# The left factors of the last pair of channel tiles on VectorE instead of GpSimd, and stored at once, in a two-layer decoder trunk on one core

## The chip, the cores and the metric

The kernel runs on one core of a Trainium2 chip. The metric is the device time of one execution in microseconds (us). The kernel before took 2596.47 us (median of three runs, 2592.08 to 2600.52). The execution that was profiled took 2591.86 us, 2590.1 us of it in the span that the trace covers. Engines are named as in the profile: PE is TensorE (PEld its weight loads), DVE VectorE, ACT ScalarE, POOL GpSimd, SP SyncE; SPq is the sequencer of SP, which issues all DMAs named below.

## What is computed

A decoder trunk of two layers over 1024 tokens of width 1024, all in float32. Each layer has an attention part and a gated convolutional FFN; the change lies in the FFN alone, which both layers have:

```python
def conv_ffn(h, w_up, conv_w, conv_b, w_down):
    u = h @ w_up
    C = u.shape[-1]
    u = lax.conv_general_dilated(u, conv_w[:, None, :], window_strides=(1,),
                                 padding=[(CONV_WIDTH - 1, 0)],
                                 dimension_numbers=('NWC', 'WIO', 'NWC'),
                                 feature_group_count=C) + conv_b
    a, b = u[..., :D_FF], u[..., D_FF:]
    return (jax.nn.silu(a) * b) @ w_down
```

`D_FF` is 2816, that is 22 channel tiles of 128.

## The kernel before

**Precision.** Every float32 product on PE is made of three matmuls on split operands (`mm3`, lines 237 to 243): each operand is split into a rounded high half (ACT copies it, line 165) and a low half (DVE subtracts, line 166), and high x high, high x low and low x high are summed in PSUM. In `mm3(out, (lh, ll), (rh, rl))` the first matmul needs both high halves, the second the low half of the right operand, the third the low half of the left operand.

**Up part.** `Up.run` works through the 22 channel tiles `n`. A table of slots (the dictionary `todo`) says when loads, sums, splits, convolution and gate of a tile are issued between its seven products on PE. `Up.gate` (line 1755) makes the hidden tile, 128 channels x 1024 tokens, as one DVE multiplication. Two tiles `g` and `h` form a pair; there are 11 pairs.

**Left factors.** The down projection is done by a seven-product scheme over 2x2 blocks (two halves of the channels, two halves of the tokens), with 11 pairs as its inner steps. Each of the seven products has a left factor per pair: `g[:, :CH]`, `h[:, :CH]`, `s2`, the in-place difference in `g[:, CH:]`, `h[:, CH:]`, `s1` and `s4` (`CH` is 512 tokens). `Up.left` makes four of them with four POOL instructions (lines 1763 to 1766); the other three are halves of the hidden tiles as they are. `Up.store` (line 1772) issues seven DMAs of 256 KB from the SP queue, which put the factors of a pair into DRAM (`gd`, one tensor per pair).

**Down part.** `Down` has 77 steps: product `i` of 7, pair `j` of 11. One step is four PSUM banks x three matmuls of 128x512, twelve matmuls. `Down.prep` loads the left factors of two pairs at a time back from DRAM (`wr<-gd`, line 1860; three buffers), and splits left factor and weight of each step (`wh`, `wl`; four buffers), three steps ahead of PE. Product 0 uses the factor `g[:, :CH]` of every pair. The first steps of product 0 are issued while the last tiles of the up part are still being convolved; its last, step 10, needs pair 10, the last that the up part makes. `Down.claim` loads the weights (`hT`, `hx`, line 1849), and `Down.sums` makes sums of weights on DVE (lines 1881, 1883, 1885) that products 2 to 6 need.

**What sets the order.** Each engine runs its instructions in order, and the SP queue issues DMAs in order: a store that waits holds up the loads behind it. Inside `Up.run` DVE and ACT keep the order in which the code is written (`tc.manual_schedule`); after it, a scheduler orders the instructions of the down part.

Of the diff's lines the ones that matter are these two slots for a pair (`n` odd), and the engine of `Up.left`:

```python
            at(7 * n + 16, self.gate, n)
            if n % 2:
                at(7 * n + 17, self.left, n // 2)
                at(7 * n + 19, self.store, n // 2)
```

Of the kernel before, what the change touches and what calls it, by code (L numbers as in the profile page):

```python
# [30 lines left out]
NF = DFF // P  # L31
# [12 lines left out]
class Plan:  # L44
# [8 lines left out]
    def add(self, eng, us, fn, deps=(), prio=0.0, acq=(), rel=()):  # L53

        t = {"eng": eng, "us": us, "fn": fn, "prio": prio, "acq": acq, "rel": rel, "id": len(self.tasks), "out": []}
        deps = {d["id"]: (d, w) for d, w in (d if isinstance(d, tuple) else (d, 0.1) for d in deps if d is not None)}
        t["wait"] = len(deps)
        for d, w in deps.values():
            d["out"].append((t, w))
        self.tasks.append(t)  # L60
        return t
# [20 lines left out]
    def run(self):  # L82
        engines = ("SP", "POOL", "DVE", "ACT", "PE")
        ready, busy = {e: [] for e in engines}, dict.fromkeys(engines, False)
        events, now, order = [], 0.0, []

        def push(t):
            heapq.heappush(ready[t["eng"]], (t["prio"], t["id"]))
        for t in self.tasks:
            if not t["wait"]:  # L90
                push(t)
        while True:
            for e in engines:
                skipped, q = [], ready[e]
                while q and not busy[e]:
                    x = heapq.heappop(q)
                    t = self.tasks[x[1]]
                    if not self.can(t):
                        skipped.append(x)
                        continue  # L100
                    self.take(t["acq"], 1)
                    order.append(t)
                    busy[e] = e != "SP"
                    heapq.heappush(events, (now + max(t["us"] - self.OVERLAP.get(e, 0.0), 0.0), 0, t["id"]))
                    heapq.heappush(events, (now + t["us"], 1, t["id"]))
                for x in skipped:
                    heapq.heappush(q, x)
            if not events:
                break
            now, kind, i = heapq.heappop(events)  # L110
            t = self.tasks[i]
            if kind == 0:
                busy[t["eng"]] = False
            elif kind == 1:
                self.take(t["rel"], -1)
                for o, w in t["out"]:
                    heapq.heappush(events, (now + w, 2, o["id"]))
            else:
                t["wait"] -= 1
                if not t["wait"]:  # L120
                    push(t)
        assert len(order) == len(self.tasks)
        for t in order:
            t["fn"]()


class Trunk:
# [422 lines left out]
    def attention(self, ap, l, od, units, work, spare, lead=4, lag=2, lead_work=2):  # L550
# [78 lines left out]
        for k in range(first, len(steps) + lag + 4):  # L629
            st = steps[k] if 0 <= k < len(steps) else None  # L630
            run(k, "max")
            if st:
                self.turn_p(ap, st)
                self.upper_p(ap, st)
            run(k, "exp")
            if st:
                self.lower_p(st)
            run(k, "norm")
            while items and items[0]["at"] <= k:
                begin(k, items.pop(0))  # L640
            if k < 0 and lead_work and items:
                for _ in range(lead_work):
                    if work:
                        advance()
            if st and k < n_fill:
                owed += max(total, 0) / (n_fill - k)
                while owed >= 1 and work:
                    owed -= 1
                    advance()
            if 0 <= k - lag < len(steps):  # L650
                for part in range(len(steps[k - lag]["t"])):
                    self.value(steps[k - lag], part)
                if steps[k - lag]["end"]:
                    finish(k, steps[k - lag]["u"])
            if not work and whole and k % 4 == 0:
                operand()
            if k == units[-1]["start"]:
                w_o = self.load_block(self.a["w_o"][l], [(0, CH)])
# [940 lines left out]
class Up:  # L1599
# [158 lines left out]
    def left(self, k):  # L1758

        g, h = self.hidden[2 * k:2 * k + 2]  # L1760
        s1, s2, s4 = (self.k.sb(self.late, [P, CH], F32, "gs", 3) for _ in range(3))
        add = self.k.nc.gpsimd.tensor_tensor
        add(s1, g[:, CH:], h[:, CH:], ALU.add)  # L1763
        add(s2, s1, g[:, :CH], ALU.subtract)
        add(g[:, CH:], g[:, :CH], g[:, CH:], ALU.subtract)
        add(s4, h[:, :CH], s2, ALU.subtract)
        self.factors = (g[:, :CH], h[:, :CH], s2, g[:, CH:], h[:, CH:], s1, s4)
# [7 lines left out]
    def run(self, late, down):  # L1775


        self.late = late
        done = {0: 3, 1: 3}
        self.split_21(1)  # L1780
        self.take_second(0)
        self.take_second(1)
        self.third(1)
        todo = {}

        def at(slot, f, *args):
            todo.setdefault(slot, []).append(lambda: f(*args))
        for slot, f in ((148, down.claim_x), (150, down.claim_x), (152, down.claim_h), (154, down.claim_h), (156, down.claim_h),
                        (158, down.claim_x), (160, down.claim_h)):
            at(slot, f)  # L1790
        at(151, down.fetch, 3)
        for slot, n in ((151, 1), (153, 2), (155, 3), (159, 4)):
            at(slot, down.prep, n)
        for n in range(NF):
            for slot, f in ((-9, self.load), (-6, self.sums_21), (-3, self.sums_34), (-3, self.split_a), (-2, self.split_21),
                            (-1, self.split_b), (3, self.split_34)):
                if n > 1 or n == 1 and f in (self.split_b, self.split_34):
                    at(7 * n + slot, f, n)
            for slot, h, tap in ((11, 0, 1), (12, 0, 0), (13, 1, 1), (14, 1, 0)):
                at(7 * n + slot, self.conv, n, h, tap)  # L1800
            at(7 * n + 16, self.gate, n)
            if n % 2:
                at(7 * n + 17, self.left, n // 2)
                at(7 * n + 19, self.store, n // 2)
        for slot in range(7 * NF + 13):
            for f in todo.pop(slot, ()):
                f()
            for n in (slot // 7 - 1, slot // 7):
                i, odd = divmod(slot - 7 * n, 2)
                if 0 <= n < NF and not odd and done.get(n, 0) <= i < 7:  # L1810
                    self.product(n, i)
            if slot >= 7 * NF + 6:
                down.step()
        assert not todo
# [157 lines left out]
```

## Time and profile before

| | us |
|---|---|
| median of three runs | 2596.47 |
| lowest and highest run | 2592.08, 2600.52 |
| profiled execution, its own time | 2591.86 |
| its span in the trace | 2590.1 |
| busy: PE | 2466.6 (95% of the span) |
| busy: DVE | 1831.0 (71%) |
| busy: ACT | 1339.8 (52%) |
| busy: POOL | 832.7 (32%) |
| DMA queue of the kernel | 43.0% of 16 engines, 355.41 MB |

The table is read from the page of the profile: its first part gives the busy times, its third the DMA queue. The chain of work that ended last is 72% PE, 6% DVE, 6% DMA, 5% ACT and 4% POOL. A busy share is an average over stages with different limits; what one change is worth is read from the stage in which it lies. The two stages here are the ends of the up part, one in each layer, near 1190 us and 2380 us of the span.

### The profile page before, as it was taken

The numbers are of one execution on the slowest core, as the hardware profiler recorded it, in microseconds if no ns is written. First come the engines' busy times: TensorE is split into PE (matmuls) and PEld (weight loads), VectorE is DVE, ScalarE is ACT, GpSimd is POOL, SyncE is SP. The second block draws the span as 40 slices with busy tenths as digits, with TensorE's granted clock in tenths as the row PEclk, the third lists the DMA queues.
The fourth block names the chain that finished last, engine by engine and source line by source line (L and its number), as shares of the span: only waits on it lengthen the run. The fifth ranks groups of instructions, "written<-read, shape, count | busy, mean of one in ns | idle before, by whom it ended". The sixth has DMA issues, their size and how long they took to land.

```text
span 2590.1 us, 35657 instructions
## 1 busy us (share of the span) xinstructions
PE 2466.6 (95%) x12306; PEld 2062.5 (80%) x12306; DVE 1831.0 (71%) x3066; ACT 1339.8 (52%) x2553; POOL 832.7 (32%) x722
## 2 busy tenths in 40 slices
PE   7889999988999999998999999999999999998998
PEld 7778888766778888886889888887777888886886
DVE  5638787666378787877665467878376888787765
ACT  5428787676244544443454356767245454443443
POOL 1335555475134554433000000000233455544000
PEclk9999999999999999999999999999999999999999
DMA  8473233244323333257335466666622333327533
GB/s 251 136 213 86 88 108 104 86 143 134 132 73 98 106 111 101 95 201 254 96 125 155 142 182 192 196 181 177 215 90 78 101 103 110 105 97 281 168 97 114
DMA packets 302700, 357.68 MB, mean 138 GB/s; under 512 B 37960, under 2 KB 183224, under 8 KB 302520
## 3 DMA queue, kind: packets, MB, share of 16 engines
q1 hardware_dynamic: 302520, 355.41, 43.0%
q8 instruction: 97, 1.59, 0.3%
q14 instruction: 83, 0.68, 0.1%
HBM read 245.55 MB, written 109.78 MB: 137 GB/s over the span
## 4 chain that ended last, share of the span: by engine, by line
PE 72%; DVE 6%; DMA 6%; ACT 5%; POOL 4%; issue 2%; SPq 1%; POOLq 0%; ACTq 0%; DVEq 0%
PE psa L241 11%; PE psa L242 11%; PE psa L243 11%; PE psb L241 8%; PE psb L243 8%; PE psb L242 8%; PE psa L384 4%; PE psb L528 4%; PE psb L504 4%; POOL gs L1763 1%; DMA hT<-in_w_down_dram 1%; ACT pt L515 1%; DVE pt L518 1%; DVE ps L414 1%; ACT ps L427 1%
## 5 line engine op out<-in xcount | busy, mean ns | idle before, releaser
L165 ACT ACTIVATE wh<-wr 128x512 fp32r<-128x512 f32 (+2 forms) x240 | 181.8, 760 | 337.1 <-PE psb L243 145.0
L1748 DVE SCALAR_TENSOR_TENSOR v<-u,cw,v 128x1023 f32<-128x1023 f32 (+1 forms) x176 | 282.8, 1607 | 68.7 <-ACT v L1746 67.1
L166 DVE TENSOR_TENSOR wl<-wr,wh 128x512 fp32r<-128x512 f32 (+2 forms) x232 | 223.5, 965 | 148.0 <-ACT wh L165 147.4
L518 DVE TENSOR_TENSOR pt<-psb,pt 128x512 fp32r<-128x512 f32 (+2 forms) x380 | 243.9, 660 | 70.9 <-ACT pt L515 69.3
L1746 ACT ACTIVATE v<-u,cw 128x1024 f32<-128x1024 f32 x88 | 109.6, 1245 | 310.0 <-DVE u L1735 283.3
L515 ACT ACTIVATE pt<-psb 128x512 fp32r<-128x512 f32 (+2 forms) x380 | 212.3, 575 | 108.3 <-PE psb L504 75.9
L528 PE MATMUL psb<-pt,vv 128*128 128x512 f32 (+2 forms) x864 | 244.6, 361 | 12.6 <-DVE pt L518 7.0
L241 PE MATMUL psa<-hT,wh 128*128 128x512 f32 x560 | 218.4, 390 | 5.3 <-DVE u L1709 5.3
L243 PE MATMUL psa<-hT,wl 128*128 128x512 f32 x560 | 218.1, 389 | 0.2 <-DVE wl L166 0.2
L242 PE MATMUL psa<-hT,wh 128*128 128x512 f32 x560 | 217.9, 389 | 0.0
L384 PE MATMUL psa<-kk,qq 128*128 128x512 f32 (+4 forms) x792 | 181.8, 349 | 23.8 <-DMA qq<-qd 11.8
L205 POOL TENSOR_TENSOR rs<-ss,consts 128x1 f32<-128x1 f32 x44 | 25.8, 589 | 503.6 <-DVE ss L203 365.3
L528 PEld LDWEIGHTS psb<-pt,vv 128*128 128x128 f32 x864 | 144.5, 190 | 34.2 <-DVE pt L518 12.2
L414 DVE CUSTOM_DVE_ANT_0 ps<-psa,caub 128x128 f32<-128x128 f32 (+1 forms) x192 | 138.9, 750 | 42.0 <-PE psa L384 37.3
L427 ACT ACTIVATE ps<-ps,stat 128x128 f32<-128x128 f32 (+1 forms) x192 | 147.5, 771 | 31.6 <-DVE stat L414 31.4
L384 PEld LDWEIGHTS psa<-kk,qq 128*128 128x128 f32 x792 | 125.6, 196 | 45.7 <-issue 18.2
L1650 POOL TENSOR_TENSOR ws<-wr 128x512 f32<-128x512 f32 x44 | 68.6, 1559 | 290.3 <-DMA wr<-in_w_up_dram 255.4
L241 PE MATMUL psb<-wh 128*128 128x512 f32 x352 | 139.7, 397 | 20.3 <-ACT wh L165 20.2
L241 PE MATMUL psb<-hT,wh 128*128 128x512 f32 x384 | 156.8, 408 | 1.0 <-ACT wh L165 0.8
L588 POOL TENSOR_TENSOR wr<-wr 128x512 f32<-128x512 f32 x16 | 21.5, 1345 | 413.4 <-DMA kd<-st 245.9
L504 PE MATMUL psb<-consts,ps 128*128 128x128 f32 x928 | 148.8, 279 | 4.5 <-POOL ps L472 2.6
L243 PE MATMUL psb<-hT,wl 128*128 128x512 f32 x384 | 152.1, 396 | 0.8 <-POOL wl L166 0.6
(306 smaller groups left out, 6906.7 us busy)
## 6 DMA issues: line engine op xcount, KB each, us to landing
wr<-in_w_up_dram SPq DMA_DIRECT2D x88, 512.0 KB
wr<-gd SPq DMA_DIRECT2D x154, 256.0 KB
gd<-v SPq DMA_DIRECT2D x88, 256.0 KB
gd<-gs SPq DMA_DIRECT2D x66, 256.0 KB
o<-ob SPq DMA_DIRECT2D x128, 128.0 KB
wr<-o SPq DMA_DIRECT2D x32, 512.0 KB
hT<-in_w_down_dram SPq DMA_DIRECT2D x64, 256.0 KB
qd<-st SPq DMA_DIRECT2D x56, 256.0 KB
```

Source lines behind the costliest of these rows:

```text
L165: nc.scalar.activation(hi, src, AF.Copy)
L166: (low or nc.vector).tensor_tensor(lo, src, f32(hi), ALU.subtract)
L241: mm(out, lh, rh, start=first, stop=False, skip_group_check=more)
L242: mm(out, lh, rl, start=False, stop=False, skip_group_check=more)
L243: mm(out, ll, rh, start=False, stop=last, skip_group_check=more)
L384: nc.tensor.matmul(out, w, rhs, start=b not in banks[:i], stop=b not in banks[i + 1:])
L427: nc.scalar.activation(p, p, AF.Exp, bias=st[:, 0, ii:ii + 1], scale=-1.0, accum_out=st[:, 1, ii:ii + 1])
L504: nc.tensor.transpose(tp[0:kb, x:x + P], br["pt"][ii][:, o:o + kb], self.ident)
L515: self.nc.scalar.activation(st["hi"], st["src"], AF.Copy)
L518: self.nc.vector.tensor_tensor(st["lo"], st["src"], f32(st["hi"]), ALU.subtract)
L528: self.nc.tensor.matmul(u["o"][:, iis[0] * P:iis[0] * P + w], br["v"](j), t[:, x:x + w], start=st["begin"] and first and i == 0, stop=st[" ...
L1748: nc.vector.scalar_tensor_tensor(v[:, d:], u[:, :S - d], cw[:, tap, i:i + 1], v[:, d:], ALU.mult, ALU.add)
```

## The change

For the last pair of each layer (`k == NF // 2 - 1`, pair 10) the four instructions of `Up.left` go to DVE instead of POOL. For that pair `left` and `store` move to the slot of `gate`, and so stand right behind the multiplication that makes the second hidden tile. The other ten pairs stay as they were.

```diff
@@ -1759,7 +1759,8 @@
 
         g, h = self.hidden[2 * k:2 * k + 2]
         s1, s2, s4 = (self.k.sb(self.late, [P, CH], F32, "gs", 3) for _ in range(3))
-        add = self.k.nc.gpsimd.tensor_tensor
+
+        add = (self.k.nc.vector if k == NF // 2 - 1 else self.k.nc.gpsimd).tensor_tensor
         add(s1, g[:, CH:], h[:, CH:], ALU.add)
         add(s2, s1, g[:, :CH], ALU.subtract)
         add(g[:, CH:], g[:, :CH], g[:, CH:], ALU.subtract)
@@ -1800,8 +1801,9 @@
                 at(7 * n + slot, self.conv, n, h, tap)
             at(7 * n + 16, self.gate, n)
             if n % 2:
-                at(7 * n + 17, self.left, n // 2)
-                at(7 * n + 19, self.store, n // 2)
+                last = n == NF - 1
+                at(7 * n + (16 if last else 17), self.left, n // 2)
+                at(7 * n + (16 if last else 19), self.store, n // 2)
```

The order of the SP queue, of PE and of ACT stays the same. On POOL the four instructions of the last pair of each layer go. On DVE the order changes behind the last `gate` of each layer. Below is DVE in layer 1, from that `gate` on, as it was before (`wl_21635` and `wl_21660` are the low halves of steps 6 and 7, `wl_21678` and `wl_21704` of steps 8 and 9, `wl_21737` of step 10; `hx<-hT` are sums of weights):

```order
L1755 TENSOR_TENSOR v_21541<-v_21541,v_21576 128x1024
L166 TENSOR_TENSOR wl_21635<-wr_21465,wh_21634 128x512
L166 TENSOR_TENSOR wl_21635<-hx_21329,wh_21634 128x512
L166 TENSOR_TENSOR wl_21660<-wr_21465,wh_21659 128x512
L166 TENSOR_TENSOR wl_21660<-hx_21329,wh_21659 128x512
L1881 TENSOR_TENSOR hx_21368<-hT_21485 128x512
L166 TENSOR_TENSOR wl_21678<-wr_21550,wh_21677 128x512
L166 TENSOR_TENSOR wl_21678<-hx_21368,wh_21677 128x512
L1881 TENSOR_TENSOR hx_21368<-hT_21516,hT_21485 128x512
```

And the same place with the change (`gs_21634`, `gs_21635`, `v_21411` and `gs_21636` are the four factors `s1`, `s2`, the in-place difference and `s4`):

```order
L1755 TENSOR_TENSOR v_21541<-v_21541,v_21576 128x1024
L1883 TENSOR_TENSOR hx_21368<-hT_21485 128x512
L1764 TENSOR_TENSOR gs_21634<-v_21411,v_21541 128x512
L1883 TENSOR_TENSOR hx_21368<-hT_21516,hT_21485 128x512
L1765 TENSOR_TENSOR gs_21635<-gs_21634,v_21411 128x512
L1766 TENSOR_TENSOR v_21411<-v_21411 128x512
L1767 TENSOR_TENSOR gs_21636<-v_21541,gs_21635 128x512
L166 TENSOR_TENSOR wl_21650<-wr_21465,wh_21649 128x512
L166 TENSOR_TENSOR wl_21650<-hx_21329,wh_21649 128x512
L166 TENSOR_TENSOR wl_21668<-wr_21465,wh_21667 128x512
L166 TENSOR_TENSOR wl_21668<-hx_21329,wh_21667 128x512
```

The four factors and two sums of weights now stand between the `gate` and the splits of step 6. Further down the same engine, with the change, this is what stands ahead of the low half of the left factor of step 10 (`wl_21737<-wr_21673`):

```order
L166 TENSOR_TENSOR wl_21737<-hx_21368,wh_21736 128x512
L1883 TENSOR_TENSOR hx_21368<-hT_21516 128x512 x2
L1883 TENSOR_TENSOR hx_21539<-hT_21516 128x512
L1883 TENSOR_TENSOR hx_21539<-hT_21567,hT_21516 128x512
L1883 TENSOR_TENSOR hx_21539<-hT_21567 128x512 x3
L1883 TENSOR_TENSOR hx_21539<-hx_21539,hT_21567 128x512
L1885 TENSOR_TENSOR hx_21329<-hx_21368,hx_21329 128x512 x4
L166 TENSOR_TENSOR wl_21737<-wr_21673,wh_21736 128x512
```

Before, twelve sums stood between these two splits as well, four of line 1881 and eight of line 1883; with the change it is eight and four, and the other four of the later kind come behind the splits of steps 10 to 15.

## Rows read from the trace of the kernel before

**Rows 1.** The page: busy time and its share of the span.

```profile
PE 2466.6 (95%) x12306; PEld 2062.5 (80%) x12306; DVE 1831.0 (71%) x3066; ACT 1339.8 (52%) x2553; POOL 832.7 (32%) x722
```

**Rows 2.** Timeline of PE (start us, us, engine line op) around step 10, both layers.

```profile
1190.40 0.39 PE L243 MATMUL psb<-wh,wl 128*128 128x512 f32 x1
1200.89 0.79 PE L241 MATMUL psb<-wh 128*128 128x512 f32 x1 [10.10 <-ACT wh L165]
...
2374.65 0.39 PE L241 MATMUL psb<-wh 128*128 128x512 f32 x1
...
2381.90 0.39 PE L243 MATMUL psb<-wh,wl 128*128 128x512 f32 x1
2392.41 0.79 PE L241 MATMUL psb<-wh 128*128 128x512 f32 x1 [10.12 <-ACT wh L165]
```

**Rows 3.** Chain of work that ended last, layer 1, 2366 to 2392 us.

```profile
2366.79 17.23 POOL gs L1763
...
2388.50 3.21 DMA wr<-gd
...
2391.73 0.64 ACT wh L165
```

**Rows 4.** Timeline of SP's DMA queue, layer 1, and its longest wait there.

```profile
2346.90 1.00 SPq L1772 DMA_DIRECT2D gd<-gs  x2
...
2362.94 5.03 SPq L1849 DMA_DIRECT2D hT<-in_w_down_dram  x8
2368.31 1.05 SPq L1772 DMA_DIRECT2D gd<-v  x2
2385.39 0.32 SPq L1772 DMA_DIRECT2D gd<-gs  x1
...
SPq L1772 <- POOL gs L1764: 15.7, 1, 15.7
```

**Rows 5.** Timeline of POOL: one earlier pair, and layer 0's last pair.

```profile
2296.87 1.29 POOL L1763 TENSOR_TENSOR gs<-v,v 128x512 f32<-128x512 f32 x1 [4.04 <-DVE v L1755]
...
1175.29 17.24 POOL L1763 TENSOR_TENSOR gs<-v,v 128x512 f32<-128x512 f32 x1 [24.94 <-DMA wr<-gd]
```

**Rows 6.** Timeline of DVE, both layers.

```profile
1186.51 4.90 DVE L1883 TENSOR_TENSOR hx<-hx,hx 128x512 f32<-128x512 f32 x8
...
2298.30 2.31 DVE L166 TENSOR_TENSOR wl<-ws,wh 128x1024 fp32r<-128x1024 f32 x1
...
2324.94 1.22 DVE L166 TENSOR_TENSOR wl<-ws,wh 128x1024 fp32r<-128x1024 f32 x1
...
2366.57 0.68 DVE L166 TENSOR_TENSOR wl<-wr,wh 128x512 fp32r<-128x512 f32 x1
...
2378.01 4.89 DVE L1883 TENSOR_TENSOR hx<-hx,hx 128x512 f32<-128x512 f32 x8
2392.39 0.69 DVE L166 TENSOR_TENSOR wl<-wr,wh 128x512 fp32r<-128x512 f32 x1 [9.49 <-ACT wh L165]
```

**Rows 7.** Windows: stretch, us, busy of PE, PEld, DVE, ACT, POOL, PEclk, DMA share, GB/s.

```profile
1200.90:1207.00 6.10, 6.10 (x17) 4.87 (x18) 4.61 (x8) 4.07 (x8) 0.00 (x0) 0.62 0.98 352
...
2366.50:2382.90 16.40, 15.79 (x70) 12.75 (x68) 16.40 (x28) 3.60 (x7) 16.12 (x1) 1.00 0.39 144
...
2372.00:2374.00 2.00, 2.00 (x11) 1.65 (x10) 2.00 (x5) 0.60 (x2) 2.00 (x1) 1.00 0.29 111
...
2392.40:2397.00 4.60, 4.59 (x11) 3.64 (x12) 4.38 (x7) 3.19 (x6) 0.00 (x0) 0.52 0.98 360
```

**Rows 8.** Two shorter gaps of PE (timeline), and the windows behind them.

```profile
1439.89 0.43 PE L1410 MATMUL psb<-lsg,tri 128*128 128x96 f32 x2 [2.61 <-issue]
...
1440.50:1444.00 3.50, 3.50 (x14) 3.50 (x13) 1.86 (x11) 0.00 (x0) 0.00 (x0) 0.58 0.77 244
...
1934.60 0.63 PE L1307 MATMUL psb<-consts,t 128*128 128x128 f32 x4 [1.03 <-DVE t L1336]
...
1934.60:1938.00 3.40, 3.40 (x19) 2.96 (x20) 3.40 (x3) 1.09 (x2) 3.40 (x3) 1.00 0.00 0
```

## The prediction

> **What bounds the kernel now.** Start with the page: PE is busy 95% of the span, DVE 71%, POOL 32% [rows 1]. Less of anything but PE pays only where PE stands still, so the next view is PE's own timeline, searched for gaps. Between 780 and 1340 us (FFN of layer 0 and what follows) and between 2330 us and the end, two gaps are over one microsecond, and both lie at the same place of the program: ahead of step 10, the last step of product 0, PE idles 10.10 us in layer 0 and 10.12 us in layer 1, each time for a split on ACT [rows 2]. They are what the change is aimed at.
>
> The chain of waits tells what that split waits for [rows 3]: POOL's first factor add takes 17.23 us, then come the other factors and the stores, then the load that step 10 needs is issued (2388.50 us) and takes 3.21 us, then ACT splits it (0.64 us). The queue of SP shows why a load of `g[:, :CH]`, which is no made factor at all, waits for POOL [rows 4]: the two stores of halves that exist went out at 2368.31 us, and the third, of `s2`, holds the in-order queue for 15.7 us until 2385.39 us. Step 10's load stands behind it.
>
> Last the question why an add of 1.29 us in an earlier pair takes 17.24 us here [rows 5]. DVE is busy without a break from the end of `gate` on, 16.40 of 16.40 us [rows 7]; its last instruction ends at 2378.01 + 4.89 = 2382.90 us, and POOL's add ends at 2384.02 us, 1.12 us later [rows 3, 6]. In layer 0 DVE's run ends at 1191.41 us and POOL's add at 1192.53 us, again 1.12 us [rows 5, 6]. I read this as POOL kept out by DVE until DVE pauses.
>
> **The change part by part.** I work on layer 1 and then transfer to layer 0. Step 10 is due on PE at 2381.90 + 0.23 = 2382.13 us; 0.23 us is the spacing of matmuls (from 2374.65 to 2381.90 us are 32 of them) [rows 2].
>
> *Removed: the wait.* Step 10 began at 2392.41 us, 10.28 us late. The gap costs more than itself: before it the granted clock was 1.00, in the 4.60 us behind it 0.52, that is mostly 1.2 instead of 2.4 GHz [rows 7]. That lost 4.60 x 0.48 = 2.2 us. Together 12.5 us. In layer 0 step 10 was due at 1190.63 us and began at 1200.89 us, 10.26 us late, and 6.10 x 0.38 = 2.3 us went to the clock [rows 2, 7]: 12.6 us.
>
> *Added on DVE: four instructions of 128x512 per layer.* The trace has the same operation on the same shape on DVE, sums of weights at 4.89 us for eight, 0.61 us each [rows 6]: 2.4 us per layer. Two sums now stand ahead of them too. So behind `gate`, instead of beginning step 6 at 2366.57 us [rows 6], DVE first does six instructions, 3.6 us, and has the low halves of step 6 at about 2371.5 us. PE's second matmul of step 6, the first that needs one, is due four steps of twelve matmuls before step 10, at 2382.13 - 48 x 0.227 + 0.23 = 2371.5 us. That is a tie; I count 0.1 us per layer. Steps 7 to 9 have at least a microsecond to spare, since each step gives PE 2.7 us of work and DVE 1.2 us.
>
> *Left over: the low half of step 10's left factor.* In DVE's order the split of the loaded factor stands behind twelve sums, as many as before. DVE had no idle time there, and its work up to this split is the same but for four factors in and four sums out. So it comes free at 2382.8 us again, the split (0.69 us) is done at 2383.5 us [rows 6], and PE's third matmul of step 10, the first that reads it, was due at 2382.13 + 2 x 0.23 = 2382.6 us. That leaves a stall of 1.0 us per layer. Does it cost clock? A gap of 1.03 us at 1934.60 us was followed by 1.00, one of 2.61 us at 1439.89 us by 0.58 [rows 8]. The stall is nearest to the first, so I take nothing; the second gives the other end, 3.5 x 0.42 = 1.5 us per layer.
>
> *Moved: the stores and the loads behind them.* With the factors made by about 2370.2 us, the third store can follow the second at 2369.4 us. But then the transfers become the limit: eight 256 KB loads before it took SP 5.03 us to issue, 0.63 us each [rows 4]. Five stores more are out by 2372.5 us, and step 10's load follows. The old traffic was through by about 2373 us (DMA share 0.29 in 2372 to 2374 us) [rows 7]. The load can land early, 2372.5 + 3.2 = 2375.7 us by its own duration [rows 3], or late, if it needs as long from there as it took from the third store on, 2391.73 - 2385.39 = 6.3 us: 2379.3 us [rows 3, 4]. With 0.64 us on ACT both are ahead of 2382.13 us. I take the late end, and no cost. The loads of steps 11 to 14 follow at 0.6 us each and have 2.7 us per step.
>
> *POOL* loses the four instructions; no later work there waits for them. The four sums that move behind step 10 are for product 2, which begins twelve steps, 32 us, later, where DVE has 1.5 us free per step.
>
> **Sum.** Layer 1: 12.5 - 1.0 - 0.1 = 11.4 us. Layer 0: 12.6 - 1.1 = 11.5 us. Together 22.9 us. PE has no gap over 0.7 us from there to the end of either down part, so all of it should reach the end: 2591.86 - 22.9 = 2569.0 us against the profiled execution. The median of the runs lies 4.6 us above that execution; against it, **2573.6 us**.
>
> **A rule that speaks against it.** The row is POOL's add, 17.23 us under an unbroken run of 27 short DVE instructions [rows 3, 7]. The converse is there as well: a DVE subtraction of 128x1024 takes 1.22 us, and 2.31 us beside POOL's adds [rows 6]. The Trainium skill, page "SBUF — State Buffer", section "Who interferes with whom", says that the port pair which both engines share is an exclusive lock, that a DVE instruction with two SBUF inputs contends for it, and that it goes to whoever issues first "for the whole instruction". By that rule POOL would get its turn after one DVE instruction, would be done by about 2368.8 us, and the 17 us would need another cause. The trace agrees that one engine holds up the other, but not that POOL gets in between two instructions. If the rule holds as written, rival 2 gains.
>
> **Rivals.**
>
> 1. *The load takes the place of POOL.* Stores and loads queue behind the last weight loads, and step 10's factor lands after 2381.4 us. For it: DMA is at its limit until about 2372 us. Against: even the late bound, 2379.3 us, leaves 2 us. If it lands at 2384 to 2387 us, PE waits 2.6 to 5.6 us and the clock falls (2.2 us): 4.8 to 7.8 us lost instead of 1.0. Saving 9.5 to 15.5 us in all: 2581 to 2587 us.
> 2. *The 17 us is a wait of the add's own data*, say for the buffers of `gs` to be stored, which the record shows inside the instruction. Then DVE inherits it, with every split behind it. `s1` would end at 2384.0 us, four more instructions and the splits of step 6 at 2387.7 us, and step 6 would stall PE by 16.2 us plus 2.2 us of clock: 18.4 instead of 12.5 us lost in each layer, 2596.5 + 2 x 5.9 = 2608 us, **slower**. It decides if the first factor on DVE takes over about 11 us. For it: the rule above. Against: the same 1.12 us behind DVE's last instruction in both layers, and the last stores of `gs` before it went out at 2346.90 us, 20 us earlier [rows 4].
> 3. *The change does not free the queue*: the third store waits for something else than POOL, for instance one of the earlier transfers, until about 2385 us. Nothing is gained, and at worst DVE's extra 2.4 us per layer shows: 2596.5 to 2601.3 us. Against: the wait of 15.7 us names POOL, and the DMA share had fallen to 0.29 by 2372 to 2374 us [rows 7].
>
> **How the numbers follow.** A measurement of this kernel tells about 0.3%, 7.8 us, from no change; the three runs differ by as much. The forecast has 0.82: its own range is 2571.4 us without any stall, less the 4.4 us by which the lowest run lies below the median, 2567 us, to 2579 us with clock lost in both layers and a little run spread. Rival 1 has 0.10, rival 2 0.03, rival 3 0.05. The first two cases end below 2588.7 us: faster 0.92; rival 3 within 0.3%: 0.05; rival 2: slower 0.03. The range 2566 to 2584 us takes in the forecast and half of rival 1.
>
> **What would show it.** In the changed kernel's trace the factor lines of the last pairs stand on DVE at about 0.6 us each; SP's third store of pair 10 comes within 2 us of the second; PE's gap ahead of step 10 is gone, with a stall of about 1 us at its third matmul, released by a `wl` split on DVE; the granted clock stays at 1.00 around it; POOL has no instruction near 17 us. I am wrong if the gap at step 10 is above 2 us with ACT waiting for a load (rival 1), if a factor on DVE lasts many microseconds (rival 2), or if the third store still goes out some 16 us after the second (rival 3).

## The result and the profile after

The changed kernel took 2569.23 us (median of four runs, 2568.14 to 2571.99), the kernel before beside it 2596.18 us (median of four, 2592.08 to 2600.52). The ratio is 0.9898, with a 95% interval of 0.9879 to 0.9916: faster by 22 to 31 us. The forecast was 2573.6 us, faster by 22.9 us. The profiled execution took 2571.99 us, 2570.2 us of it in the span.

The page after, busy times, against [rows 1]:

```profile
PE 2465.7 (96%) x12306; PEld 2062.9 (80%) x12306; DVE 1822.5 (71%) x3074; ACT 1339.1 (52%) x2553; POOL 794.5 (31%) x714
```

PE does the same work in a shorter span. DVE has eight instructions more and POOL eight fewer. POOL lost 38.2 us of busy time. Its eight instructions had taken 42.0 us in the records, twice 17.24 us and six times 1.26 us; its other instructions took 3.8 us more in this execution.

The timeline of PE around step 10 in layer 1 (start us, us, engine line op), against the gaps of 10.10 and 10.12 us in [rows 2]:

```profile
2374.17 0.39 PE L243 MATMUL psb<-wh,wl 128*128 128x512 f32 x1
2374.40 0.39 PE L241 MATMUL psb<-wh 128*128 128x512 f32 x1
2374.62 0.39 PE L242 MATMUL psb<-wl,wh 128*128 128x512 f32 x1
2374.85 0.39 PE L241 MATMUL psb<-wh 128*128 128x512 f32 x1
2375.08 0.39 PE L242 MATMUL psb<-wl,wh 128*128 128x512 f32 x1
2375.30 0.39 PE L241 MATMUL psb<-wh 128*128 128x512 f32 x1
2375.68 0.73 PE L243 MATMUL psb<-wh,wl 128*128 128x512 f32 x2
2376.24 0.40 PE L242 MATMUL psb<-wl,wh 128*128 128x512 f32 x1
```

Step 10 begins at 2374.40 us, on time. The first matmul that reads the low half of the left factor (line 243) is the sixth of the step; it is 0.15 us late, and the second of that kind, shown in the same row, another 0.11 us: 0.26 us in all. Before, the step's order was the same; these rows follow the first one of [rows 2]:

```profile
2393.00 0.63 PE L242 MATMUL psb<-wl,wh 128*128 128x512 f32 x1
2393.43 0.63 PE L241 MATMUL psb<-wh 128*128 128x512 f32 x1
2393.86 0.63 PE L242 MATMUL psb<-wl,wh 128*128 128x512 f32 x1
2394.28 0.63 PE L241 MATMUL psb<-wh 128*128 128x512 f32 x1
2394.71 1.05 PE L243 MATMUL psb<-wh,wl 128*128 128x512 f32 x2
```

The clock stays up. The windows (stretch, us, busy of PE, PEld, DVE, ACT, POOL, PEclk, DMA share, GB/s), against [rows 7]:

```profile
2357.50:2374.40 16.90, 16.90 (x76) 13.79 (x74) 16.90 (x29) 6.87 (x12) 0.00 (x0) 1.00 0.95 350
2374.40:2380.00 5.60, 5.60 (x25) 4.33 (x24) 5.60 (x11) 2.31 (x4) 0.00 (x0) 1.00 0.51 149
```

The timeline of DVE behind the last gate of layer 1, against [rows 6]; the four factors are lines 1764 to 1767:

```profile
2357.52 1.22 DVE L1755 TENSOR_TENSOR v<-v,v 128x1024 f32<-128x1024 f32 x1
2358.66 0.69 DVE L1883 TENSOR_TENSOR hx<-hT 128x512 f32<-128x512 f32 x1
2359.26 0.69 DVE L1764 TENSOR_TENSOR gs<-v,v 128x512 f32<-128x512 f32 x1
...
2361.67 0.68 DVE L1767 TENSOR_TENSOR gs<-v,gs 128x512 f32<-128x512 f32 x1
2362.27 0.68 DVE L166 TENSOR_TENSOR wl<-wr,wh 128x512 fp32r<-128x512 f32 x1
...
2374.94 0.68 DVE L166 TENSOR_TENSOR wl<-wr,wh 128x512 fp32r<-128x512 f32 x1
```

The last row is the split of step 10's left factor; it ends at 2375.62 us, 0.06 us ahead of the matmul that reads it. SP's queue, against [rows 4] (line 1773 stores, line 1862 loads):

```profile
2360.60 1.05 SPq L1773 DMA_DIRECT2D gd<-v  x2
2362.04 0.32 SPq L1773 DMA_DIRECT2D gd<-gs  x1
2362.70 1.02 SPq L1773 DMA_DIRECT2D gd<-v  x2
2363.94 1.00 SPq L1773 DMA_DIRECT2D gd<-gs  x2
2366.00 2.22 SPq L1862 DMA_DIRECT2D wr<-gd  x5
```

The third store comes 1.4 us behind the row of the first two instead of 17 us. The view of SP's waits between 2359 and 2370 us (who waits, for what: us in all, times, longest) shows what step 10's load now waits for, 1.0 us: the landing of the store of the same half.

```profile
SPq L1862 <- DMA gd<-v: 1.0, 1, 1.0
```

**The stage by itself.** From the start of the last gate to the first matmul of product 2, which begins with the first `psa<-wh` behind a gap (2428.01 us before in layer 1), the timelines give:

| us | layer 0 | layer 1 |
|---|---|---|
| before | 1173.93 to 1236.62: 62.69 | 2365.43 to 2428.01: 62.58 |
| after | 1176.89 to 1227.52: 50.63 | 2357.52 to 2408.11: 50.59 |
| gain | 12.06 | 11.99 |

Together 24.05 us. The two spans differ by 19.9 us only, because the profiled execution of the changed kernel was 3.0 us later at the first of these gates and lost 1.2 us more between the two stages, in code that is the same: 24.05 - 3.0 - 1.2 = 19.9 us.

### The profile page after: what moved, and what is told of

Its sections match the earlier page's. It is cut to its first block, busy times and chain, and to the rows that moved or that the text cites. A ratio compares the mean times of both kernels' runs of the same rounds, so it can differ in the third digit from the quotient of the medians.

```text
span 2570.2 us, 35647 instructions
## 1 busy us (share of the span) xinstructions
PE 2465.7 (96%) x12306; PEld 2062.9 (80%) x12306; DVE 1822.5 (71%) x3074; ACT 1339.1 (52%) x2553; POOL 794.5 (31%) x714
## 4 chain that ended last, share of the span: by engine, by line
PE 76%; DVE 6%; ACT 4%; DMA 4%; POOL 3%; issue 2%; SPq 0%; POOLq 0%; ACTq 0%; DVEq 0%
PE psa L241 12%; PE psa L242 12%; PE psa L243 12%; PE psb L241 9%; PE psb L243 9%; PE psb L242 9%; PE psa L384 5%; PE psb L504 4%; PE psb L528 4%; DVE pt L518 1%; ACT pt L515 1%; DVE ps L414 1%; ACT ps L427 1%; DMA wr<-o 1%; DMA wr<-in_w_up_dram 1%
## 5 line engine op out<-in xcount | busy, mean ns | idle before, releaser
L1748 DVE SCALAR_TENSOR_TENSOR v<-u,cw,v 128x1023 f32<-128x1023 f32 (+1 forms) x176 | 273.1, 1552 | 68.8 <-ACT v L1746 68.5
L1650 POOL TENSOR_TENSOR ws<-wr 128x512 f32<-128x512 f32 x44 | 77.8, 1769 | 295.7 <-DMA wr<-in_w_up_dram 251.9
L241 PE MATMUL psb<-hT,wh 128*128 128x512 f32 x384 | 156.6, 408 | 1.1 <-ACT wh L165 0.9
L242 PE MATMUL psb<-hT,wh 128*128 128x512 f32 x384 | 151.2, 394 | 0.0
```

Of the source, the lines that this page charges most:

```text
L241: mm(out, lh, rh, start=first, stop=False, skip_group_check=more)
L242: mm(out, lh, rl, start=False, stop=False, skip_group_check=more)
L1748: nc.vector.scalar_tensor_tensor(v[:, d:], u[:, :S - d], cw[:, tap, i:i + 1], v[:, d:], ALU.mult, ALU.add)
```

## The experiments

Two theories stood against each other. Theory 1: POOL's add is kept out as long as DVE runs without a pause, and the in-order queue of SP carries this to step 10. Rival: the 17 us are a wait of the add's own data. The rule that spoke against the prediction, by which POOL gets its turn behind a single DVE instruction, belongs to the rival. The slot half of the diff needs no run: with the factors on POOL and only the slots changed, the compiled order of all five engines is the one before, row for row.

### DVE in the order of the code, factors on POOL

```diff
         for n in range(down.at_step, len(down.steps)):
-            i, j = down.step()
+            if n < 33:
+                with self.tc.manual_schedule(engines={mybir.EngineType.DVE}):
+                    i, j = down.step()
+            else:
+                i, j = down.step()
```

This is the kernel before with only this edit.

> The factors of the last pair stay on POOL, as before the change; only DVE's order differs: in the down part, up to step 32, DVE keeps the order of the code, so that no sum of weights is pulled ahead of the splits. DVE then pauses between the splits of steps 7, 8 and 9, which wait for ACT. Theory 1 (POOL's add is kept out while DVE runs without a pause): the first add ends within about 4 us of the end of the gate instead of 17 us, the four factors are made some 8 us behind it, the gap of PE ahead of step 10 falls from 10.1 us to under 2 us in each layer, the clock stays at 1.00 there, and the time is 2570 to 2578 us with nothing moved to DVE. Rival (the 17 us is a wait of the add's own data or buffers, which DVE's order doesn't touch): the add still takes about 17 us, the gap stays near 10 us, the time stays at 2592 to 2600 us.

Measured: 2569.95 us (2566.21 to 2575.78), ratio 0.9901 (0.9884 to 0.9919), at the lower edge of the time expected. The timeline of POOL and, in the second fence, of DVE:

```profile
2355.95 3.43 POOL L1767 TENSOR_TENSOR gs<-v,v 128x512 f32<-128x512 f32 x1 [24.74 <-DVE v L1759]
2359.46 1.62 POOL L1768 TENSOR_TENSOR gs<-gs,v 128x512 f32<-128x512 f32 x1
```

```profile
2357.53 0.69 DVE L166 TENSOR_TENSOR wl<-hx,wh 128x512 fp32r<-128x512 f32 x1
2359.04 0.88 DVE L166 TENSOR_TENSOR wl<-wr,wh 128x512 fp32r<-128x512 f32 x1 [0.82 <-ACT wh L165]
2359.85 1.78 DVE L166 TENSOR_TENSOR wl<-hx,wh 128x512 fp32r<-128x512 f32 x1
```

DVE stops at 2358.22 us to wait for ACT, and POOL's add, begun 2.3 us earlier by the record, is done 1.2 us later, at 2359.38 us. Nothing of the add's data changed, so the rival falls. The gap at step 10 is gone with no factor on DVE. But the rows also show what theory 1 doesn't say. POOL's second add, from 2359.46 us, gets its turn behind one DVE split, the one that ends at 2359.92 us, and the next split, from 2359.85 us, is the one held up: 1.78 us instead of 0.69 us. Once POOL is in, the two engines take turns: its last two adds take 1.74 us each, and the two DVE splits beside them 1.57 and 1.78 us. This order has its own price: product 2 now begins with a gap of 1.22 us, for a split on ACT, where before and after it is 0.62 us.

### The stores that need POOL behind the loads

The kernel before, with the four stores of made factors kept back and issued at the end of `Up.run`, in code order on SP:

```diff
         for j, t in enumerate(self.factors):
-            self.k.nc.sync.dma_start(gd[j], t)
+            if k == NF // 2 - 1 and j in (2, 3, 5, 6):
+                self.rest.append((gd[j], t))
+            else:
+                self.k.nc.sync.dma_start(gd[j], t)
...
-                down.step()
+                if slot < 7 * NF + 12:
+                    down.step()
+                else:
+                    with self.k.tc.manual_schedule(engines={mybir.EngineType.SP}):
+                        down.step()
+                        for dst, t in self.rest:
+                            self.k.nc.sync.dma_start(dst, t)
```

> The factors stay on POOL, but the four stores that need POOL are issued behind the loads of steps 10 to 14 instead of ahead of them. If the in-order queue is what carries POOL's delay to step 10, the gap ahead of step 10 goes, although the factors are as late as before. The queue is then held behind the load of step 14 until POOL gets its turn, which by theory 1 is when DVE runs out of work: a new gap comes ahead of step 15, I estimate 3 to 6 us with the clock falling behind it, because five steps of 2.7 us give POOL, stores and load 13.6 us more time than before. Time 2578 to 2590 us. Rival (step 10's factor itself is late, for its load or its store, whatever stands ahead of it): the gap stays at step 10 and the time at 2592 to 2600 us.

Measured: 2577.81 us (2573.82 to 2580.49), ratio 0.9928 (0.9914 to 0.9943), just under the time expected. POOL, then SP's queue, then PE's only gap of over a microsecond in that stage, all of layer 1:

```profile
2359.42 23.29 POOL L1763 TENSOR_TENSOR gs<-v,v 128x512 f32<-128x512 f32 x1 [25.22 <-DVE v L1755]
```

```profile
2365.94 2.22 SPq L1870 DMA_DIRECT2D wr<-gd  x5
2384.10 0.32 SPq L1823 DMA_DIRECT2D gd<-gs  x1
```

```profile
2391.43 0.50 PE L241 MATMUL psa<-wh 128*128 128x512 f32 x1 [2.89 <-ACT wh L165]
```

The add takes even longer than before, 23.29 us, because DVE runs longer: its last sum ends at 2379.68 + 1.89 = 2381.57 us and the add 1.14 us later, nearly the 1.12 us of [rows 3, 6]. Step 10 isn't touched by it any more. The gap, 2.89 us (2.69 us in layer 0) where 3 to 6 us were estimated, comes five steps later, where the first load behind the held stores is due, with the granted clock at 0.70 in the 5.6 us behind it. So the delay reaches PE through the queue alone.

### Only the engine

```diff
-        add = self.k.nc.gpsimd.tensor_tensor
+        add = (self.k.nc.vector if k == NF // 2 - 1 else self.k.nc.gpsimd).tensor_tensor
```

> Only the first half of the change: the last pair's factors on DVE, but left and store in their old slots, one and three behind the gate. The factors come two DVE instructions later, behind the splits of step 6. Theory 1: the engine is all that matters; the time is that of the full change within 1 us per layer, 2567 to 2573 us; the 0.14 us that step 6 is late with the full change goes away. Rival (the early slot of the stores matters, because the queue takes them up only then): the third store comes 2 us or more later than with the full change, and the gap ahead of step 10 is 1 us or more.

Measured: 2569.1 us (2565.99 to 2571.04), ratio 0.9895 (0.988 to 0.991). The stage takes 50.56 and 50.58 us, against 50.63 and 50.59 us with both halves of the change. The 0.14 us at step 6 are gone; the remainder at step 10 is 0.41 instead of 0.26 us. The early slot brings nothing that the times can show.

### The full change with DVE in the order of the code

The edit of the first experiment on the changed kernel.

> The full change, and in the down part DVE keeps the order of the code up to step 32, so that no sum of weights stands between the splits of step 9 and of step 10. With the full change alone the low half of step 10's left factor is late by about 0.3 us and step 6 by 0.14 us. Theory 1: both go, 0.3 to 1.0 us less over the two layers, which the trace can show and the times can't: 2567 to 2573 us. Rival (sums in the order of the code collide with splits later and cost more than the early ones): gaps of PE over 0.3 us in steps 11 to 44, and a time above 2573 us.

Measured: 2570.38 us (2569.64 to 2571.36), ratio 0.9902 (0.9885 to 0.9918). Steps 6 and 10 are on time to 0.04 us, as expected. But I expected a gain, and there is none: as in the first experiment, product 2 begins behind a gap of 1.23 us instead of 0.62 us, so 0.4 us is won and 0.6 us lost in each layer. That is the kind of later gap that the rival named, but the time isn't above 2573 us. None of the versions tried is measurably faster than the change.

### A probe on POOL

The changed kernel with eight more instructions; their results are not used.

```diff
-        self.claim("h", self.k.sb(self.k.hp, [P, 8, CH], F32, "hT", 4))
+        t = self.k.sb(self.k.hp, [P, 8, CH], F32, "hT", 4)
+        self.claim("h", t)
+        self.k.nc.gpsimd.tensor_tensor(self.k.probe, t[:, 7, :P], t[:, 7, :P], ALU.add)
```

> The full change, and on POOL, idle there, one add of 128x128 behind each of the four claims of weights hT per layer. It reads the last slice of the tile just loaded and writes a tile that nobody else uses, so its only wait is the landing of that slice. It disturbs nothing that another engine waits for before step 33. The first two lie where DVE has pauses, the last two inside DVE's unbroken run behind the gate. Theory 1: the last ones take many microseconds, up to DVE's next pause, 10 us or more, the first ones under 3 us. Rival by the Trainium skill's rule (the lock is held for one instruction and given by issue order): each gets its turn behind one DVE instruction of 0.7 us and none takes over 3 us; then the 17 us before came from the add's own data.

The view of the tile `probe` (duration in ns, min, median, max), then POOL's timeline in layer 1 (the last two probes each in a window of its own), then DVE's:

```profile
L1845 POOL TENSOR_TENSOR probe<-hT x8: 402/946/9887, 1167.4 to 2371.7; 128x128 f32<-128x128 f32 x8
```

```profile
2347.31 1.40 POOL L1845 TENSOR_TENSOR probe<-hT 128x128 f32<-128x128 f32 x1 [9.52 <-DMA hT<-in_w_down_dram]
2356.00 0.47 POOL L1845 TENSOR_TENSOR probe<-hT 128x128 f32<-128x128 f32 x1 [7.29 <-DMA hT<-in_w_down_dram]
2361.98 9.61 POOL L1845 TENSOR_TENSOR probe<-hT 128x128 f32<-128x128 f32 x1 [5.50 <-DMA hT<-in_w_down_dram]
2371.67 0.73 POOL L1845 TENSOR_TENSOR probe<-hT 128x128 f32<-128x128 f32 x1
```

```profile
2370.04 0.68 DVE L166 TENSOR_TENSOR wl<-wr,wh 128x512 fp32r<-128x512 f32 x1
2370.65 1.49 DVE L166 TENSOR_TENSOR wl<-hx,wh 128x512 fp32r<-128x512 f32 x2
2372.06 0.88 DVE L1886 TENSOR_TENSOR hx<-hT 128x512 f32<-128x512 f32 x1
```

The same add takes 0.40 us at best. The one that comes just behind the start of the gate takes 9.89 us in layer 0 and 9.61 us in layer 1, where the gate starts at 2361.68 us. Its input had landed and its output tile is its own. In layer 1 it ends at 2371.59 us, where DVE has its first hitch since: the pair of splits at 2370.65 us takes 1.49 us instead of 1.31 us (the second of them needs an ACT result that is ready at about 2371.2 us, just as its turn comes). The fourth probe, ready by then, follows at once. The expectation said 10 us or more, up to DVE's next pause. The time is missed by 0.1 and 0.4 us, and what ended the wait wasn't a pause in DVE's records, which show none, but a split that was ready only just in time. Between the start of the probe and its end POOL was passed by fourteen DVE instructions behind the gate, so the rival falls here too. The run was a single one of 2576.52 us; its execution was 4.8 us behind the changed kernel's at the first of the two gates, before six of the eight probes ran, and the stage itself takes 50.96 and 50.97 us, 0.35 us more than without the probes.

## Why the prediction was right, point by point

- **The wait removed.** 12.5 and 12.6 us were to go, gap and clock. The gap went whole and the granted clock stayed at 1.00. The clock's share can be read too: from the first matmul of step 10 to product 2 it was 35.60 us before in layer 1 and is 33.71 us now, 0.26 us of that the remainder at step 10. That makes 2.15 us, where 2.2 us were counted. Right.
- **POOL kept out by DVE.** Argued from 1.12 us twice; shown for the run of DVE instructions behind the gate by the first, second and fifth run. Rival 2 is out: there the add follows what DVE does and ignores its own data. But "until DVE pauses" is no rule, and the prediction's sentence that the trace doesn't show POOL getting in between two instructions was wrong for the trace as a whole. Earlier in the up part of layer 1 POOL and, in the second fence, DVE read, before the change:

```profile
2302.98 2.29 POOL L1657 TENSOR_TENSOR ws<-wr,wr 128x512 f32<-128x512 f32 x1
2305.24 2.29 POOL L1658 TENSOR_TENSOR ws<-wr,ws 128x512 f32<-128x512 f32 x1
```

```profile
2302.53 1.57 DVE L1748 SCALAR_TENSOR_TENSOR v<-u,cw,v 128x1023 f32<-128x1023 f32 x1 [1.32 <-ACT v L1746]
2304.02 2.33 DVE L166 TENSOR_TENSOR wl<-wr,wh 128x1024 fp32r<-128x1024 f32 x1
2306.28 2.33 DVE L1748 SCALAR_TENSOR_TENSOR v<-u,cw,v 128x1022 f32<-128x1022 f32 x1
```

DVE doesn't pause here, yet each POOL add waits for one DVE instruction only (2.29 us, not 17 us), and the next DVE instruction waits for the add in turn (2.33 us, where the subtraction takes 1.22 us alone [rows 6]). So the change worked because of what the run behind the gate does. Why POOL gets no turn in that run, which is made of 128x512 instructions with two inputs in SBUF, and gets one elsewhere, no run here settles.

- **Four instructions on DVE.** 2.4 us per layer at 0.61 us each; they came at 0.60 us, and step 6 was 0.14 us late, where 0.1 us was counted.
- **Left over at step 10: the step that failed.** I took 1.0 us per layer, with the low half read by "PE's third matmul of step 10". The split was done when I said, as late as before in DVE's order. But PE's order of this step isn't that of the helper: five matmuls stand ahead of the first that reads the low half, not two. Three matmuls of 0.227 us make 0.7 us, and 1.0 - 0.7 = 0.3 us; measured 0.26 us. The rows of before, shown above, have the step in the same order, and I hadn't read on behind its first row. This makes 1.4 us over both layers; the two stages gained 24.05 us where 22.9 us were summed, 1.15 us more, so the other terms together were 0.3 us too favourable.
- **Stores and load.** The five stores were to be out 5.9 us behind the gate's end, and the load to land between 9.1 and 12.7 us behind it. The load was issued at 7.3 us (2366.00 us against 2358.66 us), later than I said, for the 1.0 us wait on its own store, which I had left out. It was split from 2370.26 us on, 11.6 us behind the gate: inside the bounds, near the late end that I chose, and 3.5 us ahead of need. Rival 1 did not come.
- **Rival 3.** The queue was freed: third store 1.4 us behind the first two.
- **The time.** 2573.6 us against 2569.23 us. Of the 4.4 us, 1.1 us is what the stages gained beyond the sum, by the step above. The rest is no mechanism that I can name: the change's four runs lie within 3.9 us, those of before within 8.4 us, and I had added the 4.6 us by which one execution differed from its median.

## What to carry to other kernels

When a POOL instruction that normally takes a microsecond shows many, look at DVE's timeline beside it before looking at its inputs. If short DVE instructions follow each other there without a break, as behind this gate, POOL may be held to the end of that run; either move the work to DVE, where it cost 0.6 us an instruction here, or give DVE another order, which gained as much in the first run. Not every busy stretch of DVE does this: in the rows at 2302.98 us POOL lost one DVE instruction and no more. Ask which in-order queue carries such a delay to PE: half of the cure is not to put what is late ahead of what is ready. And read PE's real order of a step before pricing what is late in it, since a scheduler may already have moved the matmuls that need it to the end.

## What the runs showed of the hardware

I had not expected how long POOL can be kept out. An add of 128x512 took 1.29 us alone, 17.24 us under 16.3 us of unbroken DVE instructions, and 23.29 us when that run was 6.0 us longer; one of 128x128 went from 0.40 to 9.89 us. The Trainium skill, page "SBUF — State Buffer", section "Who interferes with whom", gives the shared port pair to one instruction at a time, by issue order. The traces agree that a DVE instruction with two inputs in SBUF and a POOL instruction exclude each other. They agree with POOL's turn coming after one such instruction at 2302.98 us before the change and, in the first run, at 2359.46 us. Behind the gate they do not, and the measurement decides: there 26 DVE instructions that started after the add did went ahead of it, and it came in when DVE had nothing ready (0.8 us in the first run) or had a split whose operand was ready only just in time (the probe's). What makes the difference, and whether DVE instructions with one input would let POOL in, was not tried.
